# Two halves of 128 tokens, 2 KB apart and read alternately, as the moving operands of attention's matmuls

## The chip, the cores and the metric

One core of a Trainium2 chip runs the whole kernel. The metric is the time on the device in microseconds, the median over runs of the same program; lower is better. TensorE (PE in the profile) multiplies a stationary operand, which a weight load (PEld) brings into the array, with a moving operand that streams through column by column, and writes to PSUM. VectorE (DVE) and ScalarE (ACT) do the elementwise work, GpSimd (POOL) and SyncE (SP) mostly start DMAs.

## The reference

Two layers on 256 tokens of width 2048, inner width 4096, 32 heads of 128. Layer A is chunked attention with a learned bias by distance. Its band of 9 chunks of 64 reaches back over the whole sequence, so that every token sees all earlier chunks and its own chunk. Layer B attends causally to shared keys and values, with a forget gate's cumulative sum in the logits. Cut to what matters:

```python
# layer A
h = rms_norm(x, a_norm); q, k, v, g = split(h @ a_w_in)
o = chunked attention(q, k, v, rel_bias)          # softmax(q.k / sqrt(128) + bias) @ v, 4 chunks of 64 queries
x = x + (o * silu(g)) @ a_w_out
# layer B
h_kv = rms_norm(x, kv_norm); k, v = split(h_kv @ kv_w)
c = cumsum(log_sigmoid(h_kv @ f_w + f_b))         # per head
q, g = split(rms_norm(x, b_norm) @ b_w_in)
o = softmax(q.k / sqrt(128) + c[t] - c[s], causal) @ v   # 2 blocks of 128 queries
x = x + (o * silu(g)) @ b_w_out
return rms_norm(x, final_norm)
```

All arrays are float32.

## The kernel before

**Tokens and heads.** The 256 tokens are two tiles of 128, `t` = 0 (early) and 1 (late), `NT` = 2. Heads are worked in 16 groups of `HG` = 2 per layer, so there are 32 groups in all.

**Three matmuls for one.** To keep float32 accuracy at the faster float32r rate, operands are split into a rounded part (`hi`, `h`) by ACT and the rest (`lo`, `l`) by DVE. A product is then three matmuls: hi x hi, hi x lo and lo x hi. The helper `dot3` (lines 516 to 519) issues them; `mm3` (line 184) does the same for the projections.

**Projections** carry most of the work. The activations are stationary (128 x 128), and a stretch of weights of 2 x 256 columns moves, 512 columns to a matmul. The weights lie in SBUF as `[P, IL, KB, HN]`: the two halves (`IL` = 2) are KB x HN x 4 bytes = 2 KB apart, and `cols` (line 70) reads one column from each in turn. The host has laid out the columns so that the result stands in its usual order.

**Attention of one group** (`attention`, line 521) is a Python generator. `drive` runs it in pieces between the steps of the projection of later groups; each `yield` is such a place, and the tables of steps at the top say where it goes on. Each engine runs its instructions in the order in which they stand in its own queue. In this order:

1. `turn` brings queries and keys to head-dimension-by-token form: 32 x 32 blocks by a DVE transpose, and then 16 DMAs, from POOL's queue and in layer A also from ACT's. The blocks land in the buffer `turned`.
2. `split_pairs` (line 498) splits the keys of both tiles (tag `wide`, two heads of 256 tokens) and the late queries (tag `q1`, two heads of 128). Each half of the split is a tile of its own: `wideh`, `widel`, `q1h`, `q1l`. `feed.behind` first writes one column of each tile, from a weight buffer that is ready, so that the scheduler can't move the splits ahead of that weight.
3. Scores: `s1p` for the late queries against all 256 keys, two heads by `dot3` (six matmuls of 256 columns, lines 517 to 519). Then `s0p` for the early queries against the early keys, in full float32 (line 541), since only these tokens are visible to them.
4. Line 548 scales the scores out of PSUM and adds the bias, one DVE instruction for both heads of `s1p`, one for `s0p`. Then come the negative maximum, `Exp` on ACT with row sums, and `c`, the gate factor over the row sum. Line 562 scales the gates by it on ACT.
5. Probabilities and gates are turned by the same `turn`, through the tiles `sgY` and `sgZ` (from the tile `sg`).
6. The probabilities against the early values (both tiles of queries, 256 columns) are split into `wide` again (line 568).
7. `op`, the output: values are stationary, split probabilities move (six matmuls of 256 columns). The late queries against the late values follow in full float32 (line 575) into the second half of the same columns, `op[:, i, P:]`.
8. Line 579 multiplies with the gate and puts the result into `oT`; it is split into the stationary operand of the output projection.

The tag `wide` and others of the same pool are used at the start of the kernel too, as places for the transposed input (`homes`, line 616).

**Forget gates** (`forget`, line 790), once: 32 matmuls with the 64 columns of split gate weights as the stationary operand and the 256 tokens of the activations moving, in a row (lines 794 and 795). ACT copies the result out (line 797).

Of the kernel before, what the change touches and what calls it, by code (L numbers as in the profile page):

```python
# [9 lines left out]
F32 = mybir.dt.float32  # L10
F32R = mybir.dt.float32r
BF16 = mybir.dt.bfloat16
AF = mybir.ActivationFunctionType
OP = mybir.AluOpType
AX = mybir.AxisListType

P = 128
S = 256
NT = S // P
# [3 lines left out]
DH = 128  # L23
# [5 lines left out]
SCALE = DH ** -0.5  # L29

KD = D // P
KI = DI // P
HG = 2
# [3 lines left out]
KB = 2  # L37
IL = 2
HN = UN // IL
SQ = 32  # L40
# [25 lines left out]
def r32(ap):  # L66
    return ap.bitcast(F32)
# [8 lines left out]
def trunk(ctx, tc, x, x_t, gains, a_w_in, a_rel, a_w_out, kv_w, f_w, f_b, b_w_in, b_w_out, final_norm, out):  # L76
    nc = tc.nc
    pe, act, dve, pool, sp = nc.tensor, nc.scalar, nc.vector, nc.gpsimd, nc.sync
# [4 lines left out]
    att = ctx.enter_context(tc.tile_pool(name="att", bufs=1))  # L83
# [329 lines left out]
    feed = Feed(todo)  # L413
# [84 lines left out]
    def split_pairs(many, place=None):  # L498

        out = []  # L500
        for srcs, tag in many:
            nt = srcs[0].shape[1]
            out.append([att.tile([P, len(srcs), nt * P], F32R, name=f"{tag}{x}", tag=f"{tag}{x}") for x in "hl"])
            if place is not None:
                feed.behind(out[-1][0][:, :, :1], place)
        for k in range(len(many[0][0])):
            for (srcs, _), (hi, lo) in zip(many, out):
                h, l = (v[:, k].rearrange("p (t i u) -> p t i u", t=srcs[k].shape[1], u=SQ) for v in (hi, lo))
                act.activation(h, srcs[k], AF.Copy)
                dve.tensor_sub(l, srcs[k], r32(h))  # L510
        return out

    def split(srcs, tag, place=None):
        return split_pairs([(srcs, tag)], place)[0]
# [1 line left out]
    def dot3(out_, a, b, start=True, stop=True):  # L516
        pe.matmul(out_, a[0], b[0], start=start, stop=False)  # L517
        pe.matmul(out_, a[0], b[1], start=False, stop=False)  # L518
        pe.matmul(out_, a[1], b[0], start=False, stop=stop)  # L519

    def attention(g, biases, qk, vg, half, ocat, queues=(pool,) * NQ, line=(None, None), home=None):


        z = turn(qk.rearrange("p t (c d) -> p (t c) d", d=DH), NT * 2 * HG, "qk", queues, home)
        bias1, bias0 = biases()
        qkT = z.rearrange("p i (t c) u -> p c t i u", t=NT)
        yield
        (kh, kl), (qh, ql) = split_pairs([([qkT[:, HG + i] for i in range(HG)], "wide"),
                                          ([qkT[:, i, 1:] for i in range(HG)], "q1")], line[0])
        q0 = att.tile([P, HG, P], F32, name="q0", tag="oT")  # L530
        if line[0] is not None:
            feed.behind(q0[:, :, :1], line[0])
        act.activation(q0.rearrange("p h (i u) -> p h i u", u=SQ),
                       qkT[:, :HG, 0], AF.Copy)
        yield
        s1p = bank("s1p")[:, :].rearrange("p (i s) -> p i s", i=HG)
        s0p = bank("s0p")[:, :HG * P].rearrange("p (i s) -> p i s", i=HG)
        for i in range(HG):
            dot3(s1p[:, i], (qh[:, i], ql[:, i]), (kh[:, i], kl[:, i]))
        for i in range(HG):  # L540
            pe.matmul(s0p[:, i], q0[:, i], qkT[:, HG + i, 0], start=True, stop=True)  # L541
        NB = 1 + NT
        sg = att.tile([P, HG * NB + NT * HG, P], F32, name="sg", tag="R")
        sv = sg[:, :HG * NB].rearrange("p (i c) k -> p i (c k)", i=HG)
        nm = small.tile([P, NT, HG], F32, name="nm")
        sm = small.tile([P, NT, HG], F32, name="sm")
        for t, sp_, s_, bias in ((1, s1p, sv[:, :, P:], bias1), (0, s0p, sv[:, :, :P], bias0)):
            dve.scalar_tensor_tensor(s_, sp_, SCALE, bias, op0=OP.mult, op1=OP.add)
            dve.tensor_reduce(nm[:, t], s_, axis=AX.X, op=OP.max, negate=True)
            for i in range(HG):  # L550
                act.activation(s_[:, i], s_[:, i], AF.Exp, bias=nm[:, t, i:i + 1],
                               accum_out=sm[:, t, i:i + 1])
            if t:
                yield
        yield
        c = small.tile([P, NT, HG], F32, name="csc")
        dve.reciprocal(c, sm)
        dve.tensor_mul(c, c, half[:, :, None].to_broadcast([P, NT, HG]))
        (vh, vl, v1), gs = vg()
        for t in range(NT):  # L560
            for i in range(HG):
                act.activation(sg[:, HG * NB + t * HG + i], gs[:, t, i * DH:(i + 1) * DH], AF.Copy,
                               scale=c[:, t, i:i + 1])
        z = turn(sg, HG * NB + NT * HG, "sg")
        pT = z[:, :, :HG * NB].rearrange("p i (h c) u -> p h c i u", h=HG)
        gT = z[:, :, HG * NB:].rearrange("p i (t h) u -> p h t i u", t=NT)
        yield
        ph, pl = split([pT[:, i, :NT] for i in range(HG)], "wide", line[1])
        yield
        op = bank("op").rearrange("p (i s) -> p i s", i=HG)  # L570
        for i in range(HG):
            cols = slice(i * DH, (i + 1) * DH)
            dot3(op[:, i], (vh[:, cols], vl[:, cols]), (ph[:, i], pl[:, i]), i == 0, False)
        for i in range(HG):
            pe.matmul(op[:, i, P:], v1[:, i * DH:(i + 1) * DH], pT[:, i, NT], start=False, stop=i == HG - 1)  # L575
        yield
        oT = att.tile([P, HG, S], F32, name="oT", tag="oT")
        for i in range(HG):
            dve.tensor_mul(*(v[:, i].rearrange("p (t i u) -> p t i u", t=NT, u=SQ) for v in (oT, op)), gT[:, i])
        h0 = g * HG  # L580
        hi = ocat.hi[h0 // BIG][:, h0 % BIG:h0 % BIG + HG, :]
        lo = ocat.lo[h0 // BIG][:, h0 % BIG:h0 % BIG + HG, :]
        act.activation(hi, oT, AF.Copy)
        dve.tensor_sub(lo, oT, r32(hi))
        yield
# [27 lines left out]
    turned = big_tile([P, 2, NQ, 2 * HG * NT, SQ], F32, name="turned")  # L613
    home = [turned[:, i] for i in range(2)]
    xT = Stat("xT", KD)
    xr, homes = {}, iter(["wideh", "tb", "widel", "oT", "gs", "R", "Y", "Z", "wideh"])

    def load_xT(k0, k1):
        xr[k0] = att.tile([P, k1 - k0, S], F32, name=f"xr{k0}", tag=next(homes))
        sp.dma_start(out=xr[k0], in_=x_t[:, k0:k1])  # L620

    def split_xT(k0, k1, by_dve=False):
# [104 lines left out]
    x1T = Stat("x1T", KD)  # L727
# [62 lines left out]
    def forget():  # L790
        zp = bank("zp")[:2 * H, :S]
        for k in range(KD):
            both = fwp[:, k].rearrange("p a h -> p (a h)")
            pe.matmul(zp, both, x1T.h(k), start=k == 0, stop=False)
            pe.matmul(zp, both, x1T.l(k), start=False, stop=k == KD - 1)
        cTs = const.tile([2 * H, S], F32, name="cTs")
        act.activation(cTs, zp, AF.Copy)
        zT = cTs[:H]
        yield
        ps = bank("fps")  # L800
# [2 lines left out]
        n = NT * H  # L803
# [30 lines left out]
        for t in range(NT):  # L834
            for c in range(t + 1):
                pe.matmul(cp[:, t * H:(t + 1) * H], triu if c == t else full, w["l"][:, c * H:(c + 1) * H],
                          start=c == 0, stop=c == t)
# [150 lines left out]
```

## Time and profile before

| | us |
|---|---|
| median of 3 runs | 1761.28 (1760.0 to 1762.1) |
| the profiled execution, its own time | 1763.77 |
| span of that execution, first to last instruction | 1762.0 |
| TensorE busy | 1741.4 |
| weight loads busy | 1527.5 |
| DVE busy | 1244.3 |
| ACT busy | 1109.4 |
| POOL busy | 519.5 |

The granted TensorE clock was 0.998 over the span. In rows of the profile a line's name is followed by engine, operation and `out<-in`; `128*128` is the stationary operand and `128x256` the moving one. Rows in order of time begin with the start in us and the length in us. The length of a matmul holds its way through the array, and the next one starts before it ends; how fast matmuls follow each other is seen in the distance of their starts. A full-precision float32 matmul appears as two records.

### The profile page before, as it was taken

To read this page: it belongs to the slowest core of one execution; us is meant where nothing else is said; L and a number is where in the kernel's file an instruction comes from. 1 tells how busy PE (TensorE), PEld (TensorE's weight loads), DVE (VectorE), ACT (ScalarE), POOL (GpSimd) and SP (SyncE) were. 2 spreads that over 40 slices of the span, in tenths; PEclk is the share of its full clock that TensorE was granted. 3 is DMA by queue.
4 is the path that set the end of the run, shared out by engine and by line. 5 is a ranking of instruction groups with operands and counts; after the bars stand their busy time and mean duration, and the time that the engine had idled before them with its cause. 6 is when DMAs were issued, how large, how long until landed. Compare 5 with 4: busy or idle time off the path is not lost.

```text
span 1762.0 us, 25649 instructions
## 1 busy us (share of the span) xinstructions
PE 1741.4 (99%) x8348; PEld 1527.5 (87%) x8348; DVE 1244.3 (71%) x1818; ACT 1109.4 (63%) x2115; POOL 519.5 (29%) x1071
## 2 busy tenths in 40 slices
PE   9999999999999999998999999999999999999997
PEld 7888888888888888887888888888888888888886
DVE  7666666666666686687876777777777777876687
ACT  6555555555555566555656777777777777765454
POOL 1333333333333333212014333333333333333000
PEclk9999999999999999999999999999999999999999
DMA  8766767667677777676766777777777777777654
GB/s 299 241 223 221 226 224 223 223 225 225 224 226 228 224 224 234 196 246 208 241 218 217 238 226 226 226 226 227 226 225 224 225 225 226 229 229 239 218 201 145
DMA packets 143654, 396.35 MB, mean 225 GB/s; under 512 B 31104, under 2 KB 38560, under 8 KB 143392
## 3 DMA queue, kind: packets, MB, share of 16 engines
q1 hardware_dynamic: 107472, 354.25, 62.8%
q0 software_dynamic: 32256, 37.29, 6.5%
q10 hardware_dynamic: 3792, 3.17, 0.6%
q8 instruction: 66, 1.08, 0.2%
q14 instruction: 68, 0.56, 0.1%
HBM read 351.05 MB, written 4.23 MB: 202 GB/s over the span
## 4 chain that ended last, share of the span: by engine, by line
PE 92%; DMA 3%; DVE 2%; ACT 1%; issue 1%; POOL 1%; SPq 0%; DVEq 0%; POOLq 0%; ACTq 0%
PE bkv_acc L184 19%; PE bqg_acc L184 19%; PE aqk_acc L184 18%; PE avg_acc L184 18%; PE bo_acc L184 7%; PE ao_acc L184 4%; DMA sgZ<-sgY 1%; PE op L575 1%; PE s0p L541 1%; DMA xinZ<-xinY 1%; DVE quad_lo L295 1%; PE p L519 0%; PE p L518 0%; PE p L517 0%; PE op L518 0%
## 5 line engine op out<-in xcount | busy, mean ns | idle before, releaser
L490 POOL DMA_DIRECT2D sgZ<-sgY x512 | 251.7, 499 | 191.5 <-DVE sgY L487 112.5
L490 POOL DMA_DIRECT2D turned<-turned x448 | 220.7, 499 | 267.1 <-PE avg_acc L184 95.4
L243 DVE SCALAR_TENSOR_TENSOR bqg_lo<-bqg_raw,gain,bqg_hi 128x512 fp32r<-128x512 f32 x256 | 182.9, 752 | 83.6 <-ACT bqg_hi L242 83.3
L242 ACT ACTIVATE bqg_hi<-bqg_raw,gain 128x512 fp32r<-128x512 f32 x256 | 170.6, 714 | 104.4 <-PE bqg_acc L184 49.8
L248 DVE TENSOR_TENSOR avg_lo<-avg_raw,avg_hi 128x1024 fp32r<-128x1024 f32 x127 | 153.4, 1219 | 109.0 <-ACT avg_hi L247 107.3
L248 DVE TENSOR_TENSOR aqk_lo<-aqk_raw,aqk_hi 128x1024 fp32r<-128x1024 f32 x125 | 152.4, 1220 | 86.7 <-ACT aqk_hi L247 86.7
L243 DVE SCALAR_TENSOR_TENSOR bkv_lo<-bkv_raw,gain,bkv_hi 128x512 fp32r<-128x512 f32 x256 | 181.2, 748 | 40.9 <-ACT bkv_hi L242 38.1
L247 ACT ACTIVATE avg_hi<-avg_raw 128x1024 fp32r<-128x1024 f32 x127 | 132.5, 1056 | 120.8 <-PE aqk_acc L184 68.5
L184 PE MATMUL aqk_acc<-aqk_hi,xTh 128*128 128x512 f32 x512 | 191.1, 384 | 0.9 <-ACT aqk_hi L247 0.9
L184 PE MATMUL bqg_acc<-bqg_hi,x1Th 128*128 128x512 f32 x512 | 191.4, 384 | 0.0
L184 PE MATMUL avg_acc<-avg_hi,xTh 128*128 128x512 f32 x512 | 190.2, 382 | 0.0
L184 PE MATMUL aqk_acc<-aqk_lo,xTh 128*128 128x512 f32 x512 | 189.4, 380 | 0.7 <-DVE aqk_lo L248 0.7
L184 PE MATMUL aqk_acc<-aqk_hi,xTl 128*128 128x512 f32 x512 | 189.3, 380 | 0.0
L184 PE MATMUL bkv_acc<-bkv_hi,x1Th 128*128 128x512 f32 x512 | 189.0, 379 | 0.0
L247 ACT ACTIVATE aqk_hi<-aqk_raw 128x1024 fp32r<-128x1024 f32 x125 | 131.6, 1052 | 91.1 <-PE aqk_acc L184 43.5
L184 PE MATMUL bkv_acc<-bkv_hi,x1Tl 128*128 128x512 f32 x512 | 188.8, 379 | 0.0
L184 PE MATMUL avg_acc<-avg_hi,xTl 128*128 128x512 f32 x512 | 188.8, 379 | 0.0
L184 PE MATMUL bqg_acc<-bqg_hi,x1Tl 128*128 128x512 f32 x512 | 188.8, 379 | 0.0
L184 PE MATMUL bqg_acc<-bqg_lo,x1Th 128*128 128x512 f32 x512 | 188.8, 379 | 0.0
L184 PE MATMUL bkv_acc<-bkv_lo,x1Th 128*128 128x512 f32 x512 | 188.8, 379 | 0.0
L184 PE MATMUL avg_acc<-avg_lo,xTh 128*128 128x512 f32 x512 | 188.8, 379 | 0.0
L242 ACT ACTIVATE bkv_hi<-bkv_raw,gain 128x512 fp32r<-128x512 f32 x256 | 168.8, 712 | 25.5 <-PE bqg_acc L184 18.9
(300 smaller groups left out, 3562.6 us busy)
## 6 DMA issues: line engine op xcount, KB each, us to landing
bqg_raw<-in_b_w_in SPq DMA_DIRECT2D x128, 512.0 KB, 4.3
bkv_raw<-in_kv_w SPq DMA_DIRECT2D x128, 512.0 KB, 4.2
avg_raw<-in_a_w_in SPq DMA_DIRECT2D x127, 512.0 KB, 4.2
aqk_raw<-in_a_w_in SPq DMA_DIRECT2D x125, 512.0 KB, 4.1
ao_raw<-in_a_w_out SPq DMA_DIRECT2D x64, 512.0 KB, 4.3
bo_raw<-in_b_w_out SPq DMA_DIRECT2D x64, 512.0 KB, 4.2
sgZ<-sgY POOLq DMA_DIRECT2D x512, 40.0 KB, 4.0
turned<-turned POOLq DMA_DIRECT2D x448, 32.0 KB, 3.7
```

What stands on the lines that cost most here:

```text
L184: pe.matmul(acc[t], x[:, t * P:(t + 1) * P], w, start=t not in begun, stop=last and i == 2)
L242: act.activation(hi[:, :, j], raw[:, :, j], AF.Copy, scale=gk)
L243: dve.scalar_tensor_tensor(lo[:, :, j], raw[:, :, j], gk, r32(hi[:, :, j]), op0=OP.mult, op1=OP.subtract)
L247: act.activation(hi[:, :, j], raw[:, :, j], AF.Copy)
L248: dve.tensor_sub(lo[:, :, j], raw[:, :, j], r32(hi[:, :, j]))
L295: dve.tensor_sub(lo[:, :, :n], src, r32(hi[:, :, :n]))
L490: queues[j].dma_start(out=r32(z)[j * SQ:(j + 1) * SQ, i], in_=y[i * SQ:(i + 1) * SQ, j])
L541: pe.matmul(s0p[:, i], q0[:, i], qkT[:, HG + i, 0], start=True, stop=True)
L575: pe.matmul(op[:, i, P:], v1[:, i * DH:(i + 1) * DH], pT[:, i, NT], start=False, stop=i == HG - 1)
```

## The change

The two parts of a split now share one tile, `[P, t, 2, heads, 128]`: for each tile of tokens first the rounded part of both heads, then the rest of both heads. For keys and probabilities (two tiles of tokens, two heads) the early and late tokens of one head are then 2 x 2 x 128 x 4 bytes = 2 KB apart. The view that goes to the matmul is `p k n t`: token 0 of the early tile, token 0 of the late tile, token 1 of the early tile, and so on. Queries (one tile) are stationary and are still read in a row.

A result's columns follow the order in which the moving operand was read. So in `s1p` and `op` the early and late tokens alternate in PSUM. What reads or adds to them is changed with it:

- the biased scores are read with a step of two, in one DVE instruction for each head and no longer one for both; what is written to SBUF stands in the old order;
- the late queries' full-precision product writes every second column of `op`, `op[:, i, 1::NT]`;
- the product with the gate reads `op` with a step of two;
- `forget` reads the activations' early and late tokens alternately too, which here lie 128 x 4 = 512 bytes apart, and ACT puts the result back in order as it copies.

`xr`, the transposed input's places at the start, follows the new tags; one place (`None` in `homes`) is the second half of the tile `wide`.

```diff
         for srcs, tag in many:
-            nt = srcs[0].shape[1]
-            out.append([att.tile([P, len(srcs), nt * P], F32R, name=f"{tag}{x}", tag=f"{tag}{x}") for x in "hl"])
+            out.append(att.tile([P, srcs[0].shape[1], 2, len(srcs), P], F32R, name=tag, tag=tag))
             if place is not None:
-                feed.behind(out[-1][0][:, :, :1], place)
+                feed.behind(out[-1][:, 0, 0, :, :1], place)
         for k in range(len(many[0][0])):
-            for (srcs, _), (hi, lo) in zip(many, out):
-                h, l = (v[:, k].rearrange("p (t i u) -> p t i u", t=srcs[k].shape[1], u=SQ) for v in (hi, lo))
+            for (srcs, _), both in zip(many, out):
+                h, l = (both[:, :, i, k].rearrange("p t (i u) -> p t i u", u=SQ) for i in range(2))
                 act.activation(h, srcs[k], AF.Copy)
                 dve.tensor_sub(l, srcs[k], r32(h))
-        return out
+        return [[both[:, :, i].rearrange("p t k n -> p k n t") for i in range(2)] for both in out]
...
-            dot3(s1p[:, i], (qh[:, i], ql[:, i]), (kh[:, i], kl[:, i]))
+            dot3(s1p[:, i], (qh[:, i, :, 0], ql[:, i, :, 0]), (kh[:, i], kl[:, i]))
...
-            dve.scalar_tensor_tensor(s_, sp_, SCALE, bias, op0=OP.mult, op1=OP.add)
+            if t:
+                for i in range(HG):
+                    to, plus = (v[:, i].rearrange("p (t n) -> p t n", t=NT) for v in (s_, bias))
+                    dve.scalar_tensor_tensor(to, sp_[:, i].rearrange("p (n t) -> p t n", t=NT), SCALE, plus,
+                                             op0=OP.mult, op1=OP.add)
+            else:
+                dve.scalar_tensor_tensor(s_, sp_, SCALE, bias, op0=OP.mult, op1=OP.add)
...
-            pe.matmul(op[:, i, P:], v1[:, i * DH:(i + 1) * DH], pT[:, i, NT], start=False, stop=i == HG - 1)
+            pe.matmul(op[:, i, 1::NT], v1[:, i * DH:(i + 1) * DH], pT[:, i, NT], start=False, stop=i == HG - 1)
...
-            dve.tensor_mul(*(v[:, i].rearrange("p (t i u) -> p t i u", t=NT, u=SQ) for v in (oT, op)), gT[:, i])
+            dve.tensor_mul(oT[:, i].rearrange("p (t i u) -> p t i u", t=NT, u=SQ),
+                           op[:, i].rearrange("p (i u t) -> p t i u", t=NT, u=SQ), gT[:, i])
...
-            pe.matmul(zp, both, x1T.h(k), start=k == 0, stop=False)
-            pe.matmul(zp, both, x1T.l(k), start=False, stop=k == KD - 1)
+            hi, lo = (v.rearrange("p (t n) -> p n t", t=NT) for v in (x1T.h(k), x1T.l(k)))
+            pe.matmul(zp, both, hi, start=k == 0, stop=False)
+            pe.matmul(zp, both, lo, start=False, stop=k == KD - 1)
...
-        act.activation(cTs, zp, AF.Copy)
+        act.activation(cTs.rearrange("p (t n) -> p t n", t=NT), zp.rearrange("p (n t) -> p t n", t=NT), AF.Copy)
```

TensorE, POOL and SP hold the same instructions in the same order as before. Two queues change.

DVE, layer B, after the scores of a group: `sg<-s1p` is the biased scores, `bkv_lo` the rest of the split of a coming weight, `csc` the factor `c`. Before:

```order
L548 SCALAR_TENSOR_TENSOR sg<-s1p,cb 128x2x256
L548 SCALAR_TENSOR_TENSOR sg<-s0p,d_10565 128x2x128
L549 TENSOR_REDUCE nm<-sg 128x2 x2
L243 SCALAR_TENSOR_TENSOR bkv_lo_10784<-bkv_raw_10611,gain,bkv_hi_10783 128x2x256
L557 RECIPROCAL csc<-sm 128x4
```

After the change:

```order
L550 SCALAR_TENSOR_TENSOR sg<-s1p,cb 128x256 x2
L553 SCALAR_TENSOR_TENSOR sg<-s0p,d_10525 128x2x128
L554 TENSOR_REDUCE nm<-sg 128x2 x2
L243 SCALAR_TENSOR_TENSOR bkv_lo_10742<-bkv_raw_10570,gain,bkv_hi_10741 128x2x256
L562 RECIPROCAL csc<-sm 128x4
```

One instruction became two, in all 32 groups; nothing else on DVE moved.

ACT, layer B, after the exponentials of the same group (`sg,sm<-sg,nm`): `sg<-gs,csc` is a scaling of the gates, of which there are four, `bkv_hi` a rounded part of a coming weight, `d` and `cb` the biases of the next group. Before:

```order
L551 ACTIVATE sg,sm<-sg,nm 128x128 x2
L242 ACTIVATE bkv_hi_10805<-bkv_raw_10645,gain 128x2x256 x2
L562 ACTIVATE sg<-gs,csc 128x128
L242 ACTIVATE bkv_hi_10825<-bkv_raw_10665,gain 128x2x256 x2
L562 ACTIVATE sg<-gs,csc 128x128 x3
L858 ACTIVATE d_11020<-cb,cum 128x128 x2
L859 ACTIVATE cb<-cb,cum 128x256
```

After the change:

```order
L556 ACTIVATE sg,sm<-sg,nm 128x128 x2
L242 ACTIVATE bkv_hi_10763<-bkv_raw_10604,gain 128x2x256 x2
L242 ACTIVATE bkv_hi_10783<-bkv_raw_10624,gain 128x2x256 x2
L567 ACTIVATE sg<-gs,csc 128x128 x4
L870 ACTIVATE d_10978<-cb,cum 128x128 x2
L871 ACTIVATE cb<-cb,cum 128x256
```

The first scaling of the gates now stands behind two more weight instructions (the row `x2` that came after it), together with the other three, which keep their place. In layer A this order is as before. Beside this, SP's load of `cb` in layer B, which waited for DVE, now waits for POOL too.

More of the change, by code (lines that the diff above doesn't have):

```diff
@@ L615, in trunk @@
     xT = Stat("xT", KD)
-    xr, homes = {}, iter(["wideh", "tb", "widel", "oT", "gs", "R", "Y", "Z", "wideh"])
+    xr, homes = {}, iter(["wide", "tb", None, "oT", "gs", "R", "Y", "Z", "wide"])
     def load_xT(k0, k1):
-        xr[k0] = att.tile([P, k1 - k0, S], F32, name=f"xr{k0}", tag=next(homes))
+        home_ = next(homes)
+        if home_ is None:
+            xr[k0] = xr["wide"][:, 1]
+        else:
+            both = att.tile([P, 1 + (home_ == "wide"), KB, S], F32, name=f"xr{k0}", tag=home_)
+            xr[k0], xr[home_] = both[:, 0, :k1 - k0], both
         sp.dma_start(out=xr[k0], in_=x_t[:, k0:k1])
```

## The prediction

> **What bounds the kernel now.** I read the page first (busy shares, chain), then TensorE's waits, then its instructions in order of time.
>
> ```profile
> PE 1741.4 (99%) x8348; PEld 1527.5 (87%) x8348; DVE 1244.3 (71%) x1818; ACT 1109.4 (63%) x2115; POOL 519.5 (29%) x1071
> PE 92%; DMA 3%; DVE 2%; ACT 1%; issue 1%; POOL 1%; SPq 0%; DVEq 0%; POOLq 0%; ACTq 0%
> PE op L517 <- ACT wideh L509: 2.0, 2, 1.7
> 1077.95:1121.70 43.75, 43.75 (x213) 38.60 (x212) 31.25 (x52) 31.20 (x68) 16.56 (x34) 1.00 0.67 215
> 359.32:403.07 43.75, 43.75 (x213) 38.60 (x212) 28.24 (x37) 25.85 (x47) 13.94 (x29) 1.00 0.69 225
> ```
>
> TensorE is busy 99% of the span and holds 92% of the chain. The last two rows are one head group each (two heads; 16 groups per layer, the first row in layer B, the second in layer A): columns are the stretch, then busy time and instructions of PE, weight loads, DVE, ACT, POOL. Both take 43.75 us with PE busy throughout. So only what PE issues, and the spacing of it, can move the time; a matmul's own length (0.28 or 0.38 us) overlaps with the next, so I use distances between starts.
>
> ```profile
> 885.95 0.38 PE L184 MATMUL bqg_acc<-bqg_hi,x1Th 128*128 128x512 f32 x1
> 888.11 0.38 PE L184 MATMUL bqg_acc<-bqg_lo,x1Th 128*128 128x512 f32 x1
> 1121.70 0.28 PE L517 MATMUL s1p<-wideh,q1h 128*128 128x256 f32 x1
> 1121.82 0.28 PE L518 MATMUL s1p<-widel,q1h 128*128 128x256 f32 x1
> 1121.94 0.28 PE L519 MATMUL s1p<-wideh,q1l 128*128 128x256 f32 x1
> 1122.06 0.28 PE L517 MATMUL s1p<-wideh,q1h 128*128 128x256 f32 x1
> 1122.18 0.28 PE L518 MATMUL s1p<-widel,q1h 128*128 128x256 f32 x1
> 1122.29 0.28 PE L519 MATMUL s1p<-wideh,q1l 128*128 128x256 f32 x1
> 1122.41 0.61 PE L541 MATMUL s0p<-turned,q 128*128 128x128 f32 x4
> 1151.35 0.28 PE L517 MATMUL op<-wideh,vh 128*128 128x256 f32 x1
> 1152.06 0.61 PE L575 MATMUL op<-sgZ,v 128*128 128x128 f32 x4
> 1152.42 0.46 PE L184 MATMUL bqg_acc<-bqg_hi,x1Th 128*128 128x512 f32 x1
> 1152.72 0.38 PE L184 MATMUL bqg_acc<-bqg_lo,x1Th 128*128 128x512 f32 x1
> ```
>
> The first two rows stand ten matmuls apart: 2.16 / 10 = **216 ns** for 512 columns. These read weights through `cols`, which already takes alternate elements from two places 2 KB apart. The six score matmuls take 1122.41 - 1121.70 = 0.71 us, the six of `op` 1152.06 - 1151.35 = 0.71 us: **118.3 ns** for 256 columns read in a row. Per column that is 0.42 ns alternating and 0.46 ns contiguous; half of 216 would be 108.
>
> **The change, part by part.** (1) The 12 attention matmuls of a group read alternately. No matmul is added or removed; 32 groups x 12 = 384 change their spacing. What new spacing? From below, 108 ns, the rate of the 512-column rows. From above, 118.3, no gain. Between lies a floor by weight loads, since each matmul has its own:
>
> ```profile
> 32.49 0.36 PE L641 MATMUL ssq<-ones,sq 128*128 128x1 f32 x2
> 33.16 0.46 PE L184 MATMUL avg_acc<-avg_hi,xTh 128*128 128x512 f32 x1
> L641 PEld LDWEIGHTS ssq<-ones,sq x4: 192/192/192, 32.5 to 33.0; 128*128 128x128 f32 x4
> L517 PEld LDWEIGHTS s1p<-wideh,q1h x64: 187/188/189, 56.3 to 1605.7; 128*128 128x128 f32 x64
> 905.54 0.28 PE L795 MATMUL zp<-x1Tl,fwp 128*64 128x256 f32 x1
> 906.34 0.28 PE L794 MATMUL zp<-x1Th,fwp 128*64 128x256 f32 x1
> ```
>
> From 32.49 to 33.16 stand six records of full-precision matmuls, each with one moving column and a 128-column weight load: 0.67 / 6 = 112 ns, which can only be the loads. Attention's loads are 4 ns shorter (188 against 192), so their floor should be about 108. I take 109.5, near 108 because the 512-column rows are the same kind of matmul: 384 x (118.3 - 109.5) = **-3.4 us**; at 108 it is -4.0, at 112 -2.4, at 118.3 zero.
>
> On the reading order there is a rule. The row says 216 ns for 512 columns that change place at every element. The Trainium skill ("SBUF — State Buffer", section "Specifications (TRN2)") says that each access crossing to another 16-byte line pays a penalty, so that alternate reading would be the slow order; by it this term would be a loss and not a gain. The rows disagree for 2 KB: alternate costs less per column than contiguous.
>
> (2) The forget gates' 32 matmuls `zp` also read alternately, but their halves are 512 bytes apart. Seven steps from 905.54 to 906.34 give 0.80 / 7 = 114 ns contiguous. At 109.5 that is 32 x 4.5 = -0.1 us; if 512 bytes does nothing, 0; if it is the slow order and costs a 256-column reading twice its time, 32 x 114 = +3.6. I take -0.1, by the 2 KB rows, the nearest.
>
> (3) The late-token product, line 575 (577 after), now writes every second column of `op`. It is a full-precision matmul in two records of 128 columns: 0.36 us from 1152.06 to 1152.42 for four records, and then the next L184 row takes 0.30 instead of 0.216, so 0.444 / 4 = 111 ns each, the same as the weight-load spacing above with one column. No row here writes PSUM with a step. From below it costs nothing (a record already waits about 111 ns for its weights); from above, if a stepped write takes two turns, 128 records x 111 = +14.2 us. I take 0: the nearest rows show these records set by loads and not by columns. The accumulating 256-column products still write in a row, since the order of the columns in PSUM follows the reading.
>
> For this there is a rule against the change. The Trainium skill ("PSUM — Partial Sum Buffer", section "Specifications (TRN2)") says that PSUM lines are 8 bytes and that any non-contiguous access pattern slows matmuls significantly; no run here shows it yet, and it gives no factor. By it (3) is a loss; I make it the rival below.
>
> (4) The other engines.
>
> ```profile
> L548 DVE SCALAR_TENSOR_TENSOR sg<-s1p,cb 128x512 f32<-128x512 f32 x16 | 10.9, 684 | 1.1 <-PE s1p L519 1.1
> L548 DVE SCALAR_TENSOR_TENSOR sg<-s0p,d 128x256 f32<-128x256 f32 x16 | 6.6, 414 | 0.0
> L579 DVE TENSOR_TENSOR oT<-op,sgZ 128x256 f32<-128x256 f32 x64 | 24.1, 417 | 0.1
> L509 ACT ACTIVATE wideh<-sgZ 128x256 fp32r<-128x256 f32 x64 | 23.2, 409 | 13.1 <-DMA sgZ<-sgY 6.3 <-DMA turned<-turned 4.6
> L509 ACT ACTIVATE q1h<-turned 128x128 fp32r<-128x128 f32 x64 | 18.8, 294 | 0.0
> 1148.20 0.72 ACT L509 ACTIVATE wideh<-sgZ 128x256 fp32r<-128x256 f32 x2
> 1149.34 0.75 DVE L510 TENSOR_TENSOR widel<-sgZ,wideh 128x256 fp32r<-128x256 f32 x2
> ```
>
> The biased scores go from one DVE instruction of 512 to two of 256: 2 x 414 - 684 = +0.14 us per group; if reading PSUM at step 2 halves DVE's rate, 2 x 684 - 684 = +0.7, and the two `oT` +0.5. The splits write two pieces of 128 instead of 256 in a row: nothing at equal element counts, at most 2 x 294 - 409 = +0.2 us each. All of it is hidden: `wideh` ends at 1148.92 and `widel` at 1150.09, and PE reaches `op` only at 1151.35, 2.4 and 1.3 us later. The chain from scores to `wideh` has room as well, because `wideh` stands in ACT's queue behind weight splits that PE's buffers pace. DVE is busy 31.25 of 43.75 us and ACT 31.20. With the cover gone, 32 x 0.14 = +4.5 us at most for the scores. In layer B the first gate scaling moves behind two weight instructions on ACT; the fourth, after which DVE's transpose can start, keeps its place, so 0. Its queue holds the same instructions. SP's load of `cb` also waits for POOL now, whose masking ends before the DVE reading that the load waits for already: 0, and no weight load behind it is held.
>
> Sum: -3.4 - 0.1 + 0 + 0 = **-3.5 us**. It is made against the profiled execution:
>
> ```profile
> 1547.03 0.38 PE L517 MATMUL op<-wideh,vh 128*128 128x256 f32 x1 [1.74 <-ACT wideh L509]
> 1546.56 0.72 ACT L509 ACTIVATE wideh<-sgZ 128x256 fp32r<-128x256 f32 x2 [4.62 <-DMA turned<-turned]
> core 0: 1762.0 us, clock 0.998
> ```
>
> That execution took 1763.77 us, its span 1762.0, so 1.8 lie around it. It holds one late transfer with 1.74 us of PE idle; the median of the runs is 1761.28, 2.5 below it, so I assume that most runs lack it and that the change doesn't touch it. 1763.8 - 3.5 = 1760.3 with such a wait; from the median, **1757.8 us**.
>
> **The rivals.** *Half of it stays.* `zp` reads 256 columns in a row too, with a weight load of half the columns, and takes 114, not 118.3. So some 4.5 ns go with the length of the load, which the change leaves alone. Then spacing falls to about 114: 384 x 4.3 + 0.1 = -1.8, 1759.5 us. Against it: the 512-column rows have the same loads and show no surcharge.
>
> *It does not do what it says.* 118.3 is two back-to-back streams, moving and weights, at full duty, and the order of reading is no part of it: 0, 1761.3 us. For it: in the 512-column rows loads fill only half the time, and no row compares both orders at one width. Against it: one column with a load at full duty takes 112.
>
> *Slower: the stepped write of line 577.* If a write that fills half of a pair costs a second turn, records go from 111 to up to 222 ns: +14.2 - 3.5 = +10.7, 1772.0 us. It decides from 3.5 us / 128 = 27 ns per record upward; at 55 ns more it is +3.5, 1764.8. For it: the write port has never been used so here. Against it: a record moves 128 columns in 111 ns, 0.87 ns each, twice what a column takes in the 512-column rows, so there may be a free turn.
>
> *Slower by another's wait:* DVE's longer work surfaces in every group, +4.5 - 3.5 = +1.0, 1762.3. Against it stand the margins of 1.3 and 2.4 us.
>
> **How the numbers follow.** Forecast 0.55 (its own range 1757.0 to 1759.0, from spacings of 108 to 112), half 0.13, nothing 0.13, stepped write 0.14, surfacing waits 0.05. Within 0.2% is within 3.5 us of 1761.28, about what a measurement of this kernel can tell from no change. The forecast lies on that border: 0.31 of its 0.55 below it, 0.24 inside. Faster 0.31 + 0.02 from spread elsewhere, 0.33; slower, stepped write 0.13, waits 0.02 and spread 0.02, 0.17; same 0.50. The range, 1756.8 to 1764.0, takes in forecast, half, nothing and the surfacing waits with the 2 us by which runs differ (1760.0 to 1762.1), and leaves out the upper part of the stepped write and little below.
>
> **What would show it.** Right: score and `op` matmuls 0.65 to 0.67 us per six, a group of 43.63 to 43.68 us instead of 43.75, the four records of line 577 still 0.36 us. Half: 0.68. Nothing: 0.71. Stepped write: those four records past 0.47 us, and a group over 43.75. Waits: idle ahead of `op` in most groups, released by `wide`. The prediction is wrong if the group's length moves by anything but these matmuls.

## The result, and the profile after

| | before | after |
|---|---|---|
| median, us | 1761.38 (1758.65 to 1764.24, 22 runs) | 1758.37 (1755.80 to 1761.63, 22 runs) |
| ratio after / before | | 0.9985 [0.9978, 0.9992] |
| the profiled execution, span, us | 1762.0 | 1759.3 |

The change saves 3.0 us; the interval of the ratio allows 1.4 to 3.9. The prediction was 1757.8 us, that is 3.5 us less than the median it started from.

The page of the changed kernel, its busy shares and its chain:

```profile
PE 1737.4 (99%) x8348; PEld 1523.4 (87%) x8348; DVE 1244.0 (71%) x1850; ACT 1108.6 (63%) x2115; POOL 517.7 (29%) x1071
PE 94%; DMA 2%; DVE 2%; issue 1%; ACT 1%; POOL 1%; SPq 0%; DVEq 0%; POOLq 0%; ACTq 0%
core 0: 1759.3 us, clock 0.998
```

The bound is the same: TensorE is busy 99% of the span. It is busy 4.0 us less (1741.4 before), with the same 8348 matmuls; the spacings below account for 2.8 of it. The stretch view for one group of layer B (stretch and its length, then busy time and instructions of PE, weight loads, DVE, ACT, POOL, and last the granted clock, the share of the DMA engines and GB/s):

```profile
1074.71:1118.38 43.67, 43.67 (x213) 38.52 (x212) 31.21 (x53) 31.18 (x68) 16.51 (x34) 1.00 0.69 220
```

43.67 us stand against 43.75 before, PE busy throughout in both: 0.08 x 32 groups = 2.6 us. The rows in order of time show where in the group it comes from:

```profile
1118.38 0.27 PE L516 MATMUL s1p<-wide,q 128*128 128x256 f32 x1
1118.49 0.28 PE L517 MATMUL s1p<-wide,q 128*128 128x256 f32 x1
1118.60 0.28 PE L518 MATMUL s1p<-wide,q 128*128 128x256 f32 x1
...
1119.05 0.61 PE L540 MATMUL s0p<-turned,q 128*128 128x128 f32 x4
...
1147.99 0.27 PE L516 MATMUL op<-wide,vh 128*128 128x256 f32 x1
...
1148.65 0.61 PE L580 MATMUL op<-sgZ,v 128*128 128x128 f32 x4
1149.02 0.46 PE L184 MATMUL bqg_acc<-bqg_hi,x1Th 128*128 128x512 f32 x1
1149.32 0.38 PE L184 MATMUL bqg_acc<-bqg_lo,x1Th 128*128 128x512 f32 x1
```

and `zp`, the first and the last of its 32:

```profile
902.58 0.27 PE L806 MATMUL zp<-x1Th,fwp 128*64 128x256 f32 x1
...
905.96 0.27 PE L807 MATMUL zp<-x1Tl,fwp 128*64 128x256 f32 x1
```

The six score matmuls take 1119.05 - 1118.38 = 0.67 us and the six of `op` 0.66, where each took 0.71: about 111 ns a matmul. At the median over all groups it is 111.3, for 118.3. The late product (line 575 before, 580 now) takes 0.37 us for its four records, and the next matmul 0.30; before they took 0.36 and 0.30. The first and the last `zp` stand 31 steps apart: 3.38 / 31 = 109 ns, for 114.

On DVE the groups of the biased scores and of the product with the gate:

```profile
L550 DVE SCALAR_TENSOR_TENSOR sg<-s1p,cb 128x256 f32<-128x256 f32 x32 | 12.0, 416 | 0.2 <-PE s1p L518 0.2
L553 DVE SCALAR_TENSOR_TENSOR sg<-s0p,d 128x256 f32<-128x256 f32 x16 | 6.6, 414 | 0.0
L584 DVE TENSOR_TENSOR oT<-op,sgZ 128x256 f32<-128x256 f32 x64 | 24.0, 415 | 0.0
```

Reading PSUM with a step of two costs nothing: 416 ns for the stepped scores beside 414 for the unstepped `s0p`, and `oT` 415 for 417. The 16 instructions of layer B became 32, and their busy time went from 10.9 to 12.0 us: 0.07 us a group.

One place is not even. The stretch view of the 14th group of layer B (the 30th of 32; "the late group" below), before:

```profile
1515.48:1561.73 46.25, 44.43 (x214) 38.65 (x212) 37.91 (x69) 33.66 (x74) 16.56 (x34) 1.00 0.70 224
```

and after, in a second fence with the row of its `op` in order of time:

```profile
1511.44:1559.46 48.02, 46.12 (x214) 39.91 (x213) 37.72 (x69) 33.34 (x73) 16.52 (x34) 0.96 0.67 216
```

```profile
1543.00 0.38 PE L516 MATMUL op<-wide,vh 128*128 128x256 f32 x1 [1.79 <-ACT wide L508]
```

This is the wait that stands at 1547.03 in the profile before, which the prediction took for one late transfer of a single execution. Here it is again, in the same group: 1.79 us of idle time, and the group 48.02 us long and not 43.67. The granted clock of the stretch is 0.96 (1.00 in an undisturbed group), so part of the loss is matmuls that run slower: the stretch view gives a clock of 0.72 from 1543 to 1546 us and 0.78 from there to 1550, right behind the wait, and 1.00 ahead of it and after. In the profile before, the clock stays at 1.00 behind a wait of nearly the same length, 1.74 us.

### The profile page after: what moved, and what is told of

The parts are those of the page before. It is cut to its first block, busy times and chain, and to the rows that moved or that the text cites. A ratio compares the mean times of both kernels' runs of the same rounds, so it can differ in the third digit from the quotient of the medians.

```text
span 1759.3 us, 25696 instructions
## 1 busy us (share of the span) xinstructions
PE 1737.4 (99%) x8348; PEld 1523.4 (87%) x8348; DVE 1244.0 (71%) x1850; ACT 1108.6 (63%) x2115; POOL 517.7 (29%) x1071
## 4 chain that ended last, share of the span: by engine, by line
PE 94%; DMA 2%; DVE 2%; issue 1%; ACT 1%; POOL 1%; SPq 0%; DVEq 0%; POOLq 0%; ACTq 0%
PE bkv_acc L184 19%; PE bqg_acc L184 19%; PE avg_acc L184 18%; PE aqk_acc L184 18%; PE bo_acc L184 8%; PE ao_acc L184 5%; DMA xinZ<-xinY 1%; PE op L580 1%; PE s0p L540 1%; PE p L518 0%; PE p L516 0%; PE p L517 0%; PE op L517 0%; PE s1p L518 0%; PE s1p L517 0%
```

## The experiments

**Theory and rivals.** The theory: a float32r matmul whose moving operand is read in a row is slower than one that reads two places in turn; the place does not matter much, and weight loads set the floor. Rivals: it is the distance of 2 KB that matters, not the order; or the order is nothing, and the gain comes from the common tile or from the changed order of other engines. For the late group: its wait is made by work that stands ahead of the scores on DVE, or by one late transfer.

**Spacings, measured alone.** The changed kernel with 24 groups of 8 equal matmuls added between the layers. In the rows, `pralt` B to E are two places 512 B to 4 KB apart, `prnear` A to C the same 256 to 16 B apart, `prstep` one stream with a step, `praltH` two places with 64 weight columns, `prwide` and `prwalt` 512 columns, `prfull` and `prlong` full precision (C in a row, S and F with a stepped PSUM write, A in turn):

```diff
+    F = xT.hi[0].rearrange("p k s -> p (k s)")
+    W = xT.hi[1][:, 0, :P]
+    def alt(d):
+        return F[:, :2 * d].rearrange("p (t n) -> p n t", t=2)[:, :P]
+    def near(d):
+        return F[:, :256].rearrange("p (j t n) -> p j n t", t=2, n=d)
...
+    for o_, s_, m_ in probe("praltD", alt(512), W, "c"):
+        pe.matmul(o_, s_, m_, start=True, stop=True)
...
     x1d = dram.tile([P, NT, D], F32, name="x1d")
```

> The changed kernel with 24 runs of eight equal matmuls put in between the layers, whose results nobody reads; everything else is unchanged. Each run has one form: how the moving operand is read, how many columns the weights have, how PSUM is written. What is read is the distance of the starts inside a run. Theory (the order of reading, with a floor by weight loads): 256 columns read in a row take about 118 ns beside a load of 128 weight columns, 113 beside 64, about 111 beside 32; read alternately 111 to 112 beside 128 and 109 beside 64 and 32, so that the order and the load each have a share; 512 columns in a row take 226 or more, alternately 216. Rival (the load alone): with 32 weight columns in a row and alternately take the same, and 512 columns in a row take 216. Distance: the theory that any alternation between places at least 512 bytes apart will do expects the same 111 to 112 at 512 bytes, 1, 2 and 4 KB; the theory that 2 KB is needed expects 118 at the others. Steps of 8, 16 and 32 bytes and alternations nearer than 512 bytes are open: if every new 16-byte line cost something, 16 and 32 bytes would take more than 118. Full precision with a PSUM write at a step of two: 109 to 112 per record as with a step of one, if a stepped write is free; 200 or more if it takes a second turn.

Rows in order of time, one for each group of eight or, in full precision, sixteen records (start, length of the whole group):

```profile
709.33 1.06 PE L754 MATMUL praltB<-xTh,xTh 128*128 128x256 f32 x8
711.12 1.06 PE L758 MATMUL praltD<-xTh,xTh 128*128 128x256 f32 x8
714.69 1.06 PE L766 MATMUL prnearC<-xTh,xTh 128*128 128x256 f32 x8
715.59 1.30 PE L768 MATMUL prfour<-xTh,xTh 128*128 128x256 f32 x8
716.72 2.01 PE L770 MATMUL prstepB<-xTh,xTh 128*128 128x256 f32 x8
723.09 1.04 PE L778 MATMUL praltH<-xTh,xTh 128*64 128x256 f32 x8
725.75 2.02 PE L784 MATMUL prwide<-xTh,xTh 128*128 128x512 f32 x8
727.61 1.89 PE L786 MATMUL prwalt<-xTh,xTh 128*128 128x512 f32 x8
729.43 1.93 PE L788 MATMUL prfullC<-xTh,xTh 128*32 128x128 f32 x16
732.95 1.91 PE L792 MATMUL prfullF<-xTh,xTh 128*32 128x128 f32 x16
734.78 3.72 PE L794 MATMUL prlongC<-xTh,xTh 128*128 128x256 f32 x16
741.80 4.53 PE L798 MATMUL prlongA<-xTh,xTh 128*128 128x256 f32 x16
```

From the first of these rows to the third stand six groups, 48 matmuls: 5.36 / 48 = 111.7 ns. Means of the distances between starts within a group, without its first:

| float32r, ns | 128 weight columns | 64 | 32 |
|---|---|---|---|
| 256 columns in a row | 119.7 | 114.8 | 113.8 |
| two places in turn, 512 B, 1, 2 or 4 KB apart | 111.7 each | 109.2 (2 KB) | 109.2 (2 KB) |
| two places in turn, 256, 64 or 16 B apart | 111.7 each | | |
| four places in turn, 2 KB apart | 142.7 | | |
| one stream, step 8, 16, 32 B | 230.7, 232.8, 217.5 | | |
| 512 columns in a row; in turn, 2 KB | 231.3; 215.8 | | |

| full precision, ns a record | |
|---|---|
| 128 columns, 32 weight columns, PSUM written with step 1, 2, 4 | 109.1, 109.1, 109.2 |
| 256 columns, 128 weight columns, in a row, PSUM step 1, 2 | 215.9, 215.9 |
| 256 columns, 128 weight columns, two places in turn, 2 KB | 273.1 |

What follows. The order alone makes 8.0 ns of 119.7 here and 7.0 of 118.3 in the kernel. The distance of 2 KB is not needed: anything from 16 bytes to 4 KB does as well. Reading in turn is not good as such: with four places it is slower than in a row, and in full precision two places cost 57 ns a record. The floor is split in two by the weight columns: 109.2 ns with 64 or 32, 111.7 with 128, so 2.5 ns go with the weight load. The Trainium skill ("TensorE: Matmul & The Clock Gate", section "Wait — 56ns, not 53.3ns?") gives columns / 2.4 + 2.5 ns between starts; by that formula an estimate for 256 columns is 109.2 and for 512 it is 215.8, which are the numbers measured for reading in turn with few weight columns and for 512 columns. A stepped write to PSUM costs nothing in full precision, against the rule of the Trainium skill ("PSUM — Partial Sum Buffer", section "Specifications (TRN2)") that the prediction weighed. Float32r with a stepped PSUM write was not tried.

**The new layout, read in a row.** It keeps the common tile and its order of work and undoes the reading in turn in attention (`zp` stays as changed):

```diff
-        return [[both[:, :, i].rearrange("p t k n -> p k n t") for i in range(2)] for both in out]
+        return [[both[:, :, i].rearrange("p t k n -> p k t n") for i in range(2)] for both in out]
...
-            pe.matmul(op[:, i, 1::NT], v1[:, i * DH:(i + 1) * DH], pT[:, i, NT], start=False, stop=i == HG - 1)
+            pe.matmul(op[:, i, P:], v1[:, i * DH:(i + 1) * DH], pT[:, i, NT], start=False, stop=i == HG - 1)
```

The biased scores and the product with the gate read `s1p` and `op` as in the kernel before.

> The changed layout is kept, rounded part and rest in one tile and the halves 2 KB apart, but the matmuls read first the early half and then the late half in a row; scores, the late product and the gate are as before the change. The forget gates still read alternately. Theory (order): attention's matmuls stand 118 ns apart again, a group takes 43.75 us, and the time is that of the kernel before, less 0.1 us for the forget gates: ratio to before 0.9995 to 1.0005. Rival (it is the place of the data, or one tile for both parts): spacing 111 to 112, ratio 0.998 to 0.999.

Measured: 1761.91 us (1759.68 to 1764.72, 11 runs; before in the same series 1760.74), ratio 1.0002 [0.9993, 1.0011]. One group by the stretch view:

```profile
1075.97:1119.74 43.77, 43.77 (x213) 38.62 (x212) 30.08 (x50) 30.66 (x68) 16.52 (x34) 1.00 0.69 217
```

The gain is gone, and the group is back at 43.77 us. So it is the reading order that pays, and not the tile.

**In turn, but 512 B apart.** The tile's axes change place, so that early and late tokens of a head lie next to each other:

```diff
-            out.append(att.tile([P, srcs[0].shape[1], 2, len(srcs), P], F32R, name=tag, tag=tag))
+            out.append(att.tile([P, 2, len(srcs), srcs[0].shape[1], P], F32R, name=tag, tag=tag))
```

> The changed kernel with the early and late half of a head 512 bytes apart instead of 2 KB (the tile is ordered part, head, half, token). Read alternately as in the changed kernel. Theory (any alternation will do, as the forget gates' 109 ns at 512 bytes suggest): 111 to 112 ns, group of 43.67 us, ratio to before 0.998 to 0.999. Rival (2 KB is what counts): between 112 and 118 ns, ratio up to 1.000.

Measured: 1758.41 us (1755.9 to 1762.83, 11 runs), ratio 0.9988 [0.9979, 0.9997], and

```profile
1073.95:1117.63 43.68, 43.68 (x214) 38.52 (x212) 30.60 (x53) 30.99 (x68) 16.49 (x34) 1.00 0.72 225
```

The group is as short as with 2 KB (43.67). The distance falls as a cause.

**The late group: the sums held back.** In it the program prepares the last output projection: on DVE, sums of four blocks of the attention's result (`bo_quad`, `bo_sums`). In the order of DVE's queue they stand ahead of that group's biased scores. The edit lets them wait for a weight that is ready later, by the same trick as `split_pairs` uses:

```diff
                 k = b * KB
+                if self.name == "bo":
+                    feed.behind(xs[:, :, :1], 0)
                 dve.tensor_add(xs, r32(lhs.hi[k // BIG][:, k % BIG:k % BIG + KB]),
```

> The changed kernel, in which the sums of activations for the last projection (bo_sums) may begin only when a weight of that projection is ready, so that DVE no longer does them ahead of a group's scores. Both profiles have a PE wait of about 2 us ahead of op in the third group from the end, and DVE starts that group's biased scores 5.4 to 5.7 us after the score matmuls instead of 1.6, with four bo_sums steps in between. Theory (the sums make that wait, in every run): the wait goes, and the time falls by 2 to 4.5 us against the changed kernel, ratio to before 0.996 to 0.9975. Rival (a late transfer by chance, or one that comes back elsewhere): the ratio stays at 0.998 to 0.999, or the sums are late for the last projection and PE waits there instead.

Measured: 1757.40 us (1755.55 to 1760.01, 9 runs), ratio to before 0.9977 [0.9968, 0.9987]. That lies between the two ranges expected. The interval overlaps that of the change alone (0.9978 to 0.9992), and the 512-byte variant of the same series stands only 1.0 us higher, so both went once more side by side on one chip. In the next two expectations "layer A" is a slip: the late group is in layer B, as said above.

> The changed kernel once more, beside the next run on the same chip. Both theories (the sums make the wait ahead of the output product in layer A's last groups, or the late transfer alone does) expect 0.9978 to 0.9992 of the kernel before, that is 1757.5 to 1760 us, and 2 us or more of TensorE idle ahead of the product near 1541 us in its profile.

> The changed kernel with the sums of the bo weights held back, as in the run before, now measured against the changed kernel on the same chip. If the sums make the wait in most executions, it is 1 to 2 us below the changed kernel, and its profile has no idle time of TensorE ahead of the product near 1541 us. If the wait is one late transfer of single executions, the two agree within 0.5 us.

| same series | us | ratio to before |
|---|---|---|
| before | 1763.86 (1760.05 to 1766.28, 15 runs) | |
| the change again | 1760.13 (1758.49 to 1765.05, 11 runs) | 0.9986 [0.9977, 0.9996] |
| the change, sums held back | 1757.25 (1755.42 to 1758.58, 5 runs) | 0.9963 [0.9950, 0.9977] |

The change again: the late group by the stretch view, and then DVE's rows ahead of its biased scores and PE's at `op`, in order of time:

```profile
1511.54:1559.47 47.93, 45.69 (x213) 39.90 (x212) 38.39 (x71) 33.94 (x74) 16.49 (x34) 0.96 0.67 216
```

```profile
1511.48 0.68 DVE L371 TENSOR_TENSOR bo_quad<-oBh,oBl 128x512 f32<-128x512 f32 x1
...
1513.40 0.69 DVE L379 TENSOR_TENSOR bo_sums<-bo_quad,bo_sums 128x512 fp32r<-128x512 f32 x1
...
1516.38 0.69 DVE L371 TENSOR_TENSOR bo_quad<-oBh,oBl 128x512 f32<-128x512 f32 x1
1517.05 0.69 DVE L379 TENSOR_TENSOR bo_sums<-bo_quad,bo_sums 128x512 fp32r<-128x512 f32 x1
1517.65 0.75 DVE L550 SCALAR_TENSOR_TENSOR sg<-s1p,cb 128x256 f32<-128x256 f32 x2
1543.55 0.58 PE L516 MATMUL op<-wide,vh 128*128 128x256 f32 x1 [2.24 <-ACT wide L508]
```

With the sums held back, the same two views:

```profile
1510.29:1553.96 43.67, 43.67 (x213) 38.53 (x212) 33.59 (x57) 32.27 (x71) 16.55 (x34) 1.00 0.74 227
```

```profile
1508.70 0.42 DVE L511 TENSOR_TENSOR wide<-turned,wide 128x256 fp32r<-128x256 f32 x1
1509.04 0.29 DVE L511 TENSOR_TENSOR q<-turned,q 128x128 fp32r<-128x128 f32 x1
1509.79 3.40 DVE L243 SCALAR_TENSOR_TENSOR bkv_lo<-bkv_raw,gain,bkv_hi 128x512 fp32r<-128x512 f32 x5 [0.46 <-ACT bkv_hi L242]
1513.11 0.75 DVE L552 SCALAR_TENSOR_TENSOR sg<-s1p,cb 128x256 f32<-128x256 f32 x2
```

With the sums in front, DVE starts the biased scores 1517.65 - 1511.54 = 6.1 us after the first score matmul, and everything behind them (maximum, exponentials, turn, split) is late by as much; without them 2.8 us, and `op` finds its operand ready. The group loses 47.93 - 43.67 = 4.3 us in that profile: 2.24 of idle time, and 45.69 - 43.67 = 2.0 us of longer matmuls at a clock of 0.96. The median falls by 1760.13 - 1757.25 = 2.9 us, more than the last expectation gave the sums (1 to 2 us) and far from the agreement within 0.5 us that one late transfer of single executions would allow. But it rests on five runs on one side, and the first series, read against the 512-byte variant, gives 1.0 us.

How often the wait stands, and what sets its size, can be read from the late group in all profiles. Between the biased scores and `op`, DMAs turn the probabilities, and ACT starts the split of `op`'s operand when they have landed. In two profiles:

```profile
1518.12 0.68 DVE L547 SCALAR_TENSOR_TENSOR sg<-s1p,cb 128x512 f32<-128x512 f32 x1
1542.28 0.72 ACT L508 ACTIVATE wide<-sgZ 128x256 fp32r<-128x256 f32 x2 [2.11 <-DMA turned<-turned]
```

```profile
1543.08 0.72 ACT L508 ACTIVATE wide<-sgZ 128x256 fp32r<-128x256 f32 x2 [5.12 <-DMA sgZ<-sgY]
```

The first two rows are from the variant read in a row (its group starts at 1513.70), the last from the change again (1511.54). All profiles, counted from the group's first score matmul:

| late group, us | biased scores start | split starts | wait at `op` | length |
|---|---|---|---|---|
| read in a row | 4.4 | 28.6 | 0 | 43.83 |
| 512 B apart | 4.9 | 30.5 | 1.24 | 45.70 |
| second spacings | 4.9 | 30.8 | 1.52 | 47.66 |
| first spacings | 5.3 | 29.2 | 0.08 | 44.39 |
| the change | 5.4 | 31.1 | 1.79 | 48.02 |
| before | 5.7 | 31.1 | 1.74 | 46.25 |
| the change again | 6.1 | 31.5 | 2.24 | 47.93 |
| sums held back (two profiles) | 2.4, 2.8 | 26.4, 26.6 | 0 | 43.67 |

With the sums in front, five of seven profiles have a wait of over 1 us, so it is no accident of one execution, and it is not in all. Two things make it. The scores start 4.4 to 6.1 us into the group and not 1.6, as in the group ahead of it, and the way from there to the split takes another 23.9 to 25.9 us: in the first spacings the scores are as late as with the change, but the way is 1.8 us shorter, and the wait is all but gone. So the sums and a slow transfer are not rivals here; the sums take away the room, and what comes behind the scores, up to the landing of the transfers, decides how much is lost. Why that way varies was not found. With the sums held back even the longest way would leave room, by an estimate from the table: 2.8 + 25.9 = 28.7 us, about where the split of the variant read in a row starts without a wait. A lower clock stands behind three of the five waits (1.52, 1.79 and 2.24 us) and not behind those of 1.24 and 1.74, so what the length of a wait costs is not set by it alone.

This version, the change with the sums held back, is the fastest measured. Side by side it is 2.9 us below the change; the 1.0 us of the first series is not clear of noise, so how much it is worth stays open.

**Other orders.** What is it about reading in turn? A second set of spacings, eight matmuls for each, took words singly (`prone`), in pairs, in fours, in eights and in blocks of 32 from two places 2 KB apart, the order 0 2 1 3 (`prnearD`; that is two places in turn again, only 8 bytes apart), a row that starts 8 bytes later, two places each with a step of 8 bytes (`prtwostep`), and full precision with words in turn 64 B apart (`prfullN`):

```diff
+    def two(d, u):
+        return F[:, :2 * d].rearrange("p (t n u) -> p n t u", t=2, u=u)
```

> Eight equal matmuls in a row for each order of reading, 128 weight columns, float32r, 256 columns (240 for four places). Measured so far: in a row 119.7 ns, two places alternately 111.7 at any distance from 16 bytes up, four places 142.7, one stream with a step of 8 bytes 230.7. Theory 1, two neighbouring words one after the other are the slow pair: pairs, quads, octs and blocks of words taken alternately from two places cost 115 to 120 ns, the order 0 2 1 3 costs 111.7. Theory 2, each place is read as a stream of its own and two streams share the work: pairs, quads and octs cost 111.7 like single words, and only long blocks come near 119.7. For both: in a row from 8 bytes further on 119.7; four places 140 to 145 for 256 columns, 131 to 136 for 240; two streams that each step 8 bytes 111.7 if the step hurts only within one stream, 230 if each read costs by its line. Full precision, 256 columns: in a row 215.9, and 273 wherever two places alternate word by word; in blocks of 16 words 216 to 225.

```profile
709.53 1.05 PE L749 MATMUL prone<-xTh,xTh 128*128 128x256 f32 x8
710.42 1.53 PE L751 MATMUL prpairs<-xTh,xTh 128*128 128x256 f32 x8
711.78 1.20 PE L753 MATMUL prquads<-xTh,xTh 128*128 128x256 f32 x8
712.82 1.15 PE L755 MATMUL procts<-xTh,xTh 128*128 128x256 f32 x8
714.75 1.12 PE L759 MATMUL prnearD<-xTh,xTh 128*128 128x256 f32 x8
717.75 1.12 PE L765 MATMUL prtwostep<-xTh,xTh 128*128 128x256 f32 x8
722.16 4.53 PE L769 MATMUL prfullN<-xTh,xTh 128*128 128x256 f32 x16
```

| float32r, 256 columns, 128 weight columns | ns |
|---|---|
| in a row; from 8 bytes further on | 118.3; 120.0 |
| single words from two places in turn | 111.7 |
| pairs, fours, eights, blocks of 32 words in turn | 170.8, 129.3, 123.3, 118.8 |
| order 0 2 1 3, and so on | 119.5 |
| two places in turn, each with a step of 8 bytes | 119.0 |
| four places in turn (240 columns) | 133.3 |
| full precision: in a row; words in turn 64 B apart; fours in turn | 215.6; 273.4; 215.8 |

Both theories fall. The first (neighbours read one after the other are the slow pair) expected 115 to 120 for pairs and 111.7 for the order 0 2 1 3; measured were 170.8 and 119.5. The second (two streams share the work) expected 111.7 for pairs. Two places with a step of 8 bytes each fit neither 111.7 nor 230. Only single words from two places at least 16 bytes apart reach 111.7; 8 bytes apart, the order 0 2 1 3, they gain nothing. The row itself took 119.7 ns in the first set and 118.3 here, so differences of 1 or 2 ns between the two sets mean nothing. The full-precision row with blocks had blocks of four words and not of 16, as its expectation says. Why the order costs what it costs stays open; that it does is measured, and the tables can be used as they are.

## Why the prediction came out right, and what in it was off

**The bound.** TensorE's own spacing set the time, and what changed was the spacing of 384 + 32 matmuls. The sum of what was measured, 384 x (118.3 - 111.3) = 2.7 us and 32 x (114 - 109) = 0.16, is 2.8 us; the medians differ by 3.0. The time alone would not have told the forecast from its rival of half the gain: 1.8 us lies within the interval, and the stated range, 1756.8 to 1764.0, holds no change at all as well. The spacing tells them apart, 111.3 ns against the rival's 114.

**Part (1), mis-sized.** The step that failed is "Attention's loads are 4 ns shorter (188 against 192), so their floor should be about 108. I take 109.5". The spacing measured is 111.3 in the kernel and 111.7 alone. The 112 ns that the prediction had worked out for matmuls of one column hold for these too. The record of 188 ns was no property of the load: in the changed kernel the loads of the scores take 189 to 192, as those of one column did.

```profile
L518 PEld LDWEIGHTS s1p<-wide,q x64: 192/192/192, 56.4 to 1603.6; 128*128 128x128 f32 x64
```

The 109.5 was near what the moving side takes, 109.2 with 64 or 32 weight columns. The term is -2.7 and not -3.4 us; its bound of -2.4 for 112 ns was the nearer one.

**Part (2), right.** 109 ns at 512 bytes, -0.16 us for the -0.1 expected. Sixty-four weight columns are too few for the load to show.

**Part (3), right, for a reason that does not hold.** Records of the late product take 112.3 ns with the stepped write, beside 111.6 before and 112.1 in the variant that reads and writes in a row, and the full-precision matmuls of the first spacings give 109.1 with a step of one and of two. The prediction took these records to be "set by loads and not by columns"; but 128 columns take 109.1 ns beside 32 weight columns too, so the columns alone account for nearly all of it. The rival that cost 14.2 us is out all the same, and not because weight loads hide a slower write: with 256 columns, where columns and not loads set the time, a step of two is free as well (215.9 for both).

**Part (4), right in sign.** The split scores cost 0.07 us a group, half of the 0.14, because two instructions behind each other overlap (0.75 us for both in DVE's rows). They are hidden in every group that keeps PE busy throughout; in the late one, where DVE's queue stands on the path, they may not be, which these profiles don't separate.

**The rule on 16-byte lines.** By the Trainium skill ("SBUF — State Buffer", section "Specifications (TRN2)") reading in turn would have been the slow order. For float32r with two places it is the fast one at every distance from 16 bytes to 4 KB (111.7 against 119.7 ns). With four places (142.7 ns), and in full precision (273 against 215.9), it is slower, as a rule of that kind would have it; but pairs of words (170.8) cost more than single ones, which such a rule doesn't give.

**The wait at 1547.** "I assume that most runs lack it" is the second step that fell. The same group waits in five of the seven profiles that have the sums in front, and without the sums in neither of two. The predicted difference survived because it was taken from the median, which holds the wait wherever it stands, before and after. That "the change doesn't touch it" was assumed and not looked into: the change adds DVE work on that path, and these profiles can't tell whether the wait became longer.

**The rivals.** *Half stays* read `zp`'s 114 as a surcharge that goes with the load's length. In a row this is so (119.7, 114.8 and 113.8 ns with 128, 64 and 32 weight columns), in turn the load costs 2.5 ns and no more (111.7 against 109.2). *It does not do what it says* is out by the variant read in a row, 1.0002 of before with the tile kept. *Surfacing waits* would have shown idle time in most groups; the typical group is busy throughout.

## What to carry to other kernels

Compare the distances between matmul starts per column over all shapes of a kernel: the slow shape shows beside the fast one without any experiment, and the fast one says what is to be had, as long as weight loads leave room. Before an arrangement is chosen for float32r operands, measure a few orders in a row of equal matmuls; two places read in turn, word by word and at least 16 bytes apart, were the best of those tried, and what looks like a close relative (pairs, four places, full precision) cost up to 59 ns more. And a wait that stands once in one profile is worth a look at what lies ahead of it in the queue: here it was the program's own order that left no room, the wait stood in five of seven profiles, and moving one preparation was worth 1.0 us in one series and 2.9 in the other, beside the 3.0 of the change itself.

## What the runs showed of the hardware that was not expected

- A float32r matmul that reads its moving operand in a row is not at the full rate: 119.7 ns for 256 columns and 231.3 for 512, against 111.7 and 215.8 with two places in turn. For 256 columns the places may be 16 bytes apart; 8 bytes apart the gain is gone (119.5).
- A single stream with a step of 8 to 32 bytes takes about twice the time (217 to 233 ns); two such streams of 8 bytes in turn take 119.0.
- Pairs of words from two places cost 170.8 ns, more than single words (111.7) and more than fours (129.3).
- In full precision it is the other way round: in a row 215.9 ns a record, two places word by word 273, in fours 215.8.
- A weight load of 128 columns shows with 2.5 ns in a matmul of 256 columns that are read in turn, and with 5 ns where they are read in a row (119.7 against 114.8 with 64 weight columns).
- Behind a wait of 1.5 to 2.2 us of TensorE late in the kernel the granted clock fell in three profiles (0.72 and 0.78 in the 7 us behind the wait of 1.79 us), and stayed at 1.00 in another behind 1.74 us.
